# Six preparation tasks and two gate rows moved from the end of the input projection into attention steps 6 to 25

## The chip, the cores and the metric

The kernel runs on one core of one Trainium2 chip. The metric is the device time of one execution in microseconds (us). The core's engines are named as in the profile: PE (TensorE, matrix products; PEld its weight loads), DVE (VectorE), ACT (ScalarE), POOL (GpSimd) and SP (SyncE, which here only issues DMAs). Each engine works through its own queue in order. ACT issues DMAs as well, out of the same queue as its arithmetic.

## The reference

One step of a one-layer encoder over 1024 prompt frames and 32 sample frames, 1056 rows in all, in fp32, with a width of 1024:

```python
h = rmsnorm(x, g_mix)
q, k, v, cb, cc, cx, ga, gc = split(h @ w_in)        # 3 x 512, 3 x 512, 2 x 1024 columns
y_attn = stick_breaking(q, k, v) @ w_attn_out         # 8 heads x 64, strictly causal
y_conv = (cb * causal_conv(cc * cx)) @ w_conv_out
merged = sigmoid(ga) * y_attn + sigmoid(gc) * y_conv
x = x + merged @ w_o
x = x + square(relu(rmsnorm(x, g_ffn) @ w_up)) @ w_down
x = x + sigmoid(rmsnorm(x, g_ple) @ w_ple_gate) * (p @ w_ple)
y = rmsnorm(x, g_final)
# stick_breaking: A[t,s] = beta[t,s] * prod over s<j<t of (1 - beta[t,j]), beta = sigmoid(q k / 8)
```

The outputs are `y` and the new keys, values and convolution rows. The sample frames attend to 256 cached frames as well.

## The kernel before

Activations lie with features on the 128 partitions and the 1056 rows in the free dimension. A product in fp32 precision is made of three faster ones: each operand is split into a high part (a cast on ACT to `fp32r`) and a low part (the rest, a subtraction on DVE), and high x high, high x low and low x high are summed in PSUM. The larger products are cut into 2 x 2 blocks and done with seven block products in place of eight (`seven`).

The stages follow one another: input projection (column sets `SETS`, 0 to 17), attention, the two branches with their gates, output projection, MLP up and down, and the last gated addition. PE has work in nearly all of it. The order on ACT, PE, DVE and POOL is that of the program text (`manual_schedule(engines=MM)`); DMAs issued on SP are placed by the framework.

**The input projection.** `run(seven(...))` makes one set of two 128-column blocks; at each of its `yield`s every generator in the list `side` is advanced by one piece. `after(n, g)` lets n turns go by first. The last set, 17, is gate rows 6 and 7; `last_m` keeps its two tiles unscaled. A short piece of other PE work (`START`) and the rest of `side` follow, and then the attention.

**The six tasks.** `ahead_gate(n)` (n = 4, 5) loads raw gate row n from `gd`, lets four more turns go by, multiplies it by the row norm `rs` (`scaled`, DVE, 128x1056), takes the sigmoid on ACT, and stores it to `gs_` with a DMA that ACT issues. `ahead_attn(n)` (n = 4 to 7) loads weight row n of `w_attn_out` (256 KB), splits it some turns later (ACT cast and DVE subtraction, 128x512), and two turns after that stores both halves to `aod` (512 KB, issued by ACT). The branches read `gs_` and `aod` after the attention.

**The attention.** The prompt is done in 64 steps: 4 pairs of heads x 2 heads x 8 blocks of 128 queries. Step n with block i = n mod 8 has 128(i+1) keys. The loop `for n in range(LAST + 3)` runs a pipeline over three steps, in the order `ORDER = "LSAFBFG"`:

- L: DVE scan along the keys of step n-1 (`weigh`, `remains`), and leftovers of `pending`
- S: `scores(n)`: PE products into the PSUM tile `z`, which has one buffer; sigmoid on ACT from `z` to `r` (L865); POOL sets the masked corner of `r`
- A and B: `flip(n-2)`: PE transposes of `r`, high part by ACT (L918), low part by DVE (L919), into tiles `at`
- F: other PE work (gate rows 0 to 3, embedding, convolution branch), cut into pieces; `shares()` allots it to the steps beforehand
- G, in odd blocks: `gather(n-3)`, PE products of weights and values into `av`

At the top of an even step SP gets the loads of the queries for step n+4 (`queries`, three DMAs), and at i = 2 the keys and values of the next head (`keys_values`). Steps 1 to 14 carry the sample frames' attention too (`sample_loads`, `samples`).

In the kernel before, the two kept rows of `last_m` are scaled at the top of steps 3 and 4, and pass the sigmoid and are stored at the top of steps 5 and 6.

Most large tiles, operands, gate rows, `at`, keys and values, the tiles of the six tasks and the kept rows, share one pool, `bpool`, with `NBUF = 34` buffers of 128 x 1056 fp32.

Of the kernel before, what the change touches and what calls it, by code (L numbers as in the profile page):

```python
# [11 lines left out]
AF = mybir.ActivationFunctionType  # L12
# [32 lines left out]
ORDER = "LSAFBFG"  # L45
START = 2.5
SQ_AT = 96
AHEAD = 6
MM = {mybir.EngineType.Activation, mybir.EngineType.PE, mybir.EngineType.DVE, mybir.EngineType.Pool}


# [1 line left out]
def tile_step(  # L53
# [8 lines left out]
    nc = tc.nc  # L62
# [7 lines left out]
    def blk(name, dt=F32, shape=None):  # L70
        return bpool.tile(shape or [P, T], dt, tag="B", name=name)
# [13 lines left out]
    for m_, a_, b_ in ((keep, 1.0, 0.0), (drop, 0.0, 1.0)):  # L85
        nc.gpsimd.memset(m_, a_)
        for p_ in range(4):
            r_ = m_[32 * p_ : 32 * p_ + 32, :]
            nc.gpsimd.affine_select(
                r_, r_, pattern=[[-1, DEC]], compare_op=ALU.is_gt, fill=b_, base=0, channel_multiplier=1  # L90
# [51 lines left out]
    raws, ws, side = {}, {}, []  # L142
# [174 lines left out]
    def after(n, *gens):  # L317
        for _ in range(n):
            yield
        for g in gens:  # L320
            yield from g

    def call(f, *a):
        f(*a)
        yield

    def run(body):

        for _ in body:
            for g in list(side):  # L330
                if next(g, g) is g:
                    side.remove(g)
# [4 lines left out]
    SETS = [("g", 12), ("g", 4)] + [(nm, 0) for nm in ("cc", "cx", "cb", "q", "k", "v")] + [("g", 8)]  # L337
# [115 lines left out]
    def stats_x():  # L453

        nc.vector.memset(ssq, 1.0)
        for i in range(9):
            n = P if i < 8 else DEC
            r = rows[i % 3][:n, :]
            nc.scalar.activation(r, r, AF.Square, accum_out=ssq[:n, i : i + 1])
            if i < 6:  # L460
                load_rows(i + 3)
            for _ in range(3 if i in (2, 5) else 1):
                yield
        nc.scalar.activation(rst, ssq, AF.Sqrt, bias=eps_t, scale=1.0 / D)
        nc.vector.reciprocal(rst, rst)
        for _ in range(3):
            yield
        for q0 in (0, 3, 6):
            spread(rst, rs, q0)


    gd = dpool.tile([16, P, T], F32, name="gd")
# [53 lines left out]
    def scaled(m, by=None):  # L526
        if by is None:
            dve(m, m, rs, op=ALU.mult)
        else:
            nc.vector.scalar_tensor_tensor(m, m, by, rs, op0=ALU.mult, op1=ALU.mult)  # L530
# [97 lines left out]
    def ahead_attn(n):  # L628
        t = blk(f"ao{n}", F32R, [P, 2, 4, P])
        raw = t[:, 1].bitcast(F32)  # L630
        nc.sync.dma_start(raw, w_attn_out[n])
        for _ in range(5):
            yield
        nc.scalar.copy(t[:, 0], raw)
        dve(t[:, 1], raw, t[:, 0].bitcast(F32), op=sub)
        yield
        yield
        nc.scalar.dma_start(aod[n], t.bitcast(F32).rearrange("p e k n -> p e (k n)"))
        yield

    def ahead_gate(n):
        m = blk(f"ga{n}")
        nc.sync.dma_start(m, gd[n])
        for _ in range(5):
            yield
        scaled(m)
        yield
        nc.scalar.activation(m, m, AF.Sigmoid)
        nc.scalar.dma_start(gs_[n - 4], m)
        yield  # L650
# [55 lines left out]
    def second_parts(a):  # L706

        r = blk(f"xb{a}", F32, [P, 2, TH])
        for i in range(2):
            nc.sync.dma_start(r[:, i, :], xf[4 * a + 2 * i][:, TH:])  # L710
        for _ in range(4):
            yield
        for i in range(2):
            j = 2 * a + i
            d, g = operand("B12", j), gmix[:, 2 * j : 2 * j + 1]
            nc.scalar.activation(d[:, 0, :], r[:, i, :], AF.Copy, scale=g)
            mix(d[:, 1, :], r[:, i, :], g, d[:, 0, :].bitcast(F32), sub)
            yield
# [125 lines left out]
    def queries(p, j, c):  # L844
        q = live["q", p, j, c] = apool.tile([P, 2, 256], F32R, tag="Q", name=f"q{p}{j}{c}", bufs=3)
        src = qd[p, 64 * j : 64 * j + 64, :, c * 256 : (c + 1) * 256]
        nc.sync.dma_start(q[0:64, :, :].bitcast(F32), src)
        nc.sync.dma_start(q[64:128, 0, :].bitcast(F32), src[:, 1, :])
        nc.sync.dma_start(q[64:128, 1, :].bitcast(F32), src[:, 0, :])
# [36 lines left out]
    def weigh(p, j, i):  # L886
        remains(*live[p, j, i])
# [337 lines left out]
    with tc.manual_schedule(engines=MM):  # L1225
        nc.scalar.preload_act_table_set("sqrt_and_others")
        run(first_gates())
        for s_ in range(2, len(SETS)):
            nm, n = SETS[s_]
            if s_ == 2:  # L1230
                side.append(after(1, stats_x()))
            elif s_ == 4:
                nc.scalar.preload_act_table_set("sigmoid_and_others")
            elif s_ == len(SETS) - 1:
                side.extend(after(AHEAD + i // 2, ahead_gate(n)) for i, n in enumerate((4, 5)))
                side.extend(after(AHEAD + 1 + i // 2, ahead_attn(n)) for i, n in enumerate(range(4, 8)))
            if s_ + 1 < len(SETS):
                side.append(prepare(f"i{s_ + 1}", AT_IN))
            else:
                side.extend([after(4, second_parts(0)), after(6, second_parts(1)), after(4, call(hooks_to, -20)), after(10, call(hooks_to, 0))])  # L1240
            if s_ + 2 < len(SETS):
                side.append(after(5, call(fetch_in, s_ + 2)))
            m = blk(f"m1_i{s_}"), blk(f"m2_i{s_}")
            run(seven(f"i{s_}", *m, copy_of))
            if s_ + 1 < len(SETS):
                follow(nm, n, m, 6 * (s_ == 2))
            else:
                last_m = n, m
        keys_values(0, 0)
        pools[:] = [gps]  # L1250
        run(ahead(START))
        while side:
            run(range(1))
# [99 lines left out]
    with tc.manual_schedule(engines=MM):  # L1353
        queries(0, 0, 0)
        queries(0, 0, 1)
        for n in range(LAST + 3):
            done_f, parts = 0, None
            if n in (3, 4):
                scaled(last_m[1][n - 3])
            elif n in (5, 6):  # L1360
                m = last_m[1][n - 5]
                nc.scalar.activation(m, m, AF.Sigmoid)
                nc.scalar.dma_start(gd[last_m[0] + n - 5], m)
            if n == 1:
                sample_loads()
            elif n == 3:
                sample_keys()
            if n < LAST:
                i = steps[n][2]
                if i % 2 == 0 and n + 4 < LAST:  # L1370
                    p_, j_, i_ = steps[n + 4]
                    queries(p_, j_, i_ // 2)
                if i == 2 and n + 8 < LAST:
                    keys_values(*steps[n + 8][:2])
            for op in ORDER:
                if op == "S" and n < LAST:
                    scores(*steps[n])
                    if n == LAST - 1:
                        zf = zps.tile([P, 2, 512], F32, tag="z", name="zf")
                        spare_ps.extend(zf[:, h, :] for h in range(2))  # L1380
                elif op == "L":
                    if 1 <= n <= LAST:
                        weigh(*steps[n - 1])
                    for f in pending + split_low:
                        f()
                    pending.clear()
                    split_low.clear()
                elif op == "F" and n < LAST + 2:
                    done_f += 1
                    fill(share[n] + (share[n + 1] - share[n]) * done_f / nf)  # L1390
                    if done_f == 1 and n in SAMPLE_AT:
                        next(sample, None)
                elif op == "G" and n >= 3 and steps[n - 3][2] % 2 == 1:
                    p, j, i_ = steps[n - 3]
                    gather(p, j, i_ // 2)
                elif op in "AB" and 2 <= n <= LAST + 1:
                    if op == "A":
                        parts = flip(*steps[n - 2])
                    next(parts, None)
            for p, c in splits.get(n, ()):  # L1400
                split_high(p, c)
            branches_ahead(n)
            if n == LAST + 1:
                fill(2 * total)
                hooks_to(len(plan))
                split_high(3, slice(0, 768))
        for f in pending + split_low:
            f()
        split_high(3, slice(768, T))
        split_low.pop()()  # L1410
# [997 lines left out]
```

## Time and profile before

| | us |
|---|---|
| median of 3 runs | 1540.46 |
| lowest, highest | 1539.76, 1541.39 |
| profiled execution, its own time | 1543.13 |
| span of the profiled execution | 1541.4 |

| stretch of the profiled execution | from, to (us) |
|---|---|
| issue of the loads of the six tasks (SP) | 384.6 to 390.3 |
| their arithmetic (DVE, ACT) | 396.3 to 403.8 |
| first and last scores on PE | 403.0, about 605 |
| scores of step 8 | 434.6 |

The span runs from the first instruction's start to the last one's end. Rows of a timeline are: start, duration, engine, line, operation, output tile <- inputs, shape; a bracket gives the time for which the engine stood idle before it and what ended that. "DMA" in a row of stretches is the busy share of the 16 DMA engines.

### The profile page before, as it was taken

What the parts mean: (1) busy time and instruction counts of PE and PEld (TensorE: products, weight loads), DVE (VectorE), ACT (ScalarE), POOL (GpSimd) and SP (SyncE); (2) the same over time, 40 slices, a digit from 0 to 9 for tenths busy, and PEclk for the clock granted to TensorE, in tenths of its full rate; (3) what the DMA queues carried; (4) which work ended last, traced back from release to release, by engine and by line L of the source; (5) the groups of instructions that cost most, each with busy time, mean ns of one, the idle gap of its engine ahead of it and who ended that gap; (6) DMA issues with size and microseconds to landing.
All of it is one profiled execution on the core that took longest, in us unless ns stands there. A gap on an engine that the chain in (4) does not pass through costs nothing.

```text
span 1541.4 us, 29904 instructions
## 1 busy us (share of the span) xinstructions
PE 1511.6 (98%) x11888; PEld 1498.2 (97%) x11888; DVE 1131.5 (73%) x1597; ACT 763.0 (50%) x1415; POOL 280.9 (18%) x318
## 2 busy tenths in 40 slices
PE   8999999999899999999999999999999999999997
PEld 8999999999789999999999999999999999999997
DVE  7568666657578988799876677675576986799756
ACT  6544444434456666333375556645543334434654
POOL 2123322231012212000002113222020220000253
PEclk9999999999999999999999999999999999999999
DMA  6513445413946752446755455544886897673443
GB/s 223 202 51 114 190 153 193 166 45 132 311 133 191 253 164 92 168 162 224 267 182 173 159 171 209 193 154 154 300 282 200 277 332 240 205 274 121 140 127 118
DMA packets 121036, 286.83 MB, mean 186 GB/s; under 512 B 13856, under 2 KB 34592, under 8 KB 120896
## 3 DMA queue, kind: packets, MB, share of 16 engines
q1 hardware_dynamic: 119456, 280.34, 54.3%
q10 hardware_dynamic: 1440, 4.58, 0.7%
q8 instruction: 93, 1.52, 0.4%
q14 instruction: 47, 0.39, 0.1%
HBM read 200.98 MB, written 83.89 MB: 185 GB/s over the span
## 4 chain that ended last, share of the span: by engine, by line
PE 59%; DVE 2%; ACT 1%; issue 1%; DMA 0%; SPq 0%; DVEq 0%; ACTq 0%
PE ps_dn L1993 7%; PE ps_dn L1991 7%; PE ps_dn L1992 7%; PE ps_woA L1709 4%; PE ps_A11u L244 2%; PE ps_A11u L242 2%; PE ps_A11u L243 2%; PE ps_pg L120 2%; PE ps_pg L121 2%; PE ps_pg L122 2%; PE ps_S1u L243 2%; PE ps_S1u L244 2%; PE ps_S1u L242 2%; PE ps_woS L1709 2%; PE ps_oa L120 1%; PE ps_oa L122 1%
## 5 line engine op out<-in xcount | busy, mean ns | idle before, releaser
L1993 PE MATMUL ps_dn<-fh,wlo_dn 128*128 128x264 f32 x896 | 255.4, 285 | 0.0
L1992 PE MATMUL ps_dn<-fl,whi_dn 128*128 128x264 f32 x896 | 254.9, 284 | 0.0
L1991 PE MATMUL ps_dn<-fh,whi_dn 128*128 128x264 f32 x896 | 254.8, 284 | 0.0
L1991 PEld LDWEIGHTS ps_dn<-fh,whi_dn 128*128 128x128 f32 x896 | 168.9, 188 | 0.0
L1993 PEld LDWEIGHTS ps_dn<-fh,wlo_dn 128*128 128x128 f32 x896 | 168.8, 188 | 0.0
L1992 PEld LDWEIGHTS ps_dn<-fl,whi_dn 128*128 128x128 f32 x896 | 168.6, 188 | 0.0
L209 POOL TENSOR_TENSOR s_u<-raw_u,raw_u 128x512 f32<-128x512 f32 x22 | 32.1, 1461 | 359.6 <-DVE slS_u L170 284.6
L879 DVE TENSOR_TENSOR_SCAN r<-r 128x128 f32<-128x128 f32 (+3 forms) x64 | 86.5, 1351 | 2.8 <-POOL r L872 2.8
L209 POOL TENSOR_TENSOR s_i<-raw_i,raw_i 128x512 f32<-128x512 f32 x32 | 44.2, 1380 | 239.4 <-DVE slS_i L170 210.3
L1878 ACT CAST whi_dn<-raw_dn 128x1024 fp32r<-128x1024 f32 x40 | 42.0, 1051 | 84.9 <-PE ps_dn L1992 80.9
L1884 DVE TENSOR_TENSOR wlo_dn<-raw_dn,whi_dn 128x1024 fp32r<-128x1024 f32 x40 | 60.9, 1523 | 29.0 <-ACT whi_dn L1878 28.9
L919 DVE TENSOR_TENSOR at<-pa,at 128x512 fp32r<-128x512 f32 (+2 forms) x96 | 52.0, 550 | 31.5 <-ACT at L918 26.9
L242 PE MATMUL ps_A11i<-T,shS_i 128*128 128x264 f32 x256 | 73.1, 286 | 0.0
L244 PE MATMUL ps_A11i<-T,slS_i 128*128 128x264 f32 x256 | 73.0, 285 | 0.0
L243 PE MATMUL ps_A11i<-T,shS_i 128*128 128x264 f32 x256 | 72.8, 284 | 0.0
L170 DVE TENSOR_TENSOR slS_i<-s_i,shS_i 128x512 fp32r<-128x512 f32 x48 | 34.8, 731 | 50.0 <-ACT shS_i L168 49.9
L1904 DVE TENSOR_TENSOR fl<-mr,fh 128x1056 fp32r<-128x1056 f32 x56 | 69.9, 1247 | 0.0
L1753 ACT ACTIVATE m<-m 128x528 f32<-128x528 f32 (+1 forms) x52 | 31.8, 611 | 74.6 <-DVE m L289 30.4
L872 POOL TENSOR_SCALAR_AFFINE_SELECT r<-r 128x128 f32<-128x128 f32 x64 | 30.4, 475 | 201.6 <-ACT r L865 191.4
L2075 POOL TENSOR_TENSOR xx<-xx,pgs 128x384 f32<-128x384 f32 (+1 forms) x23 | 24.2, 1056 | 216.5 <-DVE pgs L2074 209.9
L170 DVE TENSOR_TENSOR slS_u<-s_u,shS_u 128x512 fp32r<-128x512 f32 x48 | 34.3, 715 | 39.8 <-ACT shS_u L168 39.8
L1899 ACT CAST fh<-mr 128x1056 fp32r<-128x1056 f32 x56 | 60.1, 1073 | 0.3 <-DMA mr<-mdB 0.3
(568 smaller groups left out, 5699.0 us busy)
## 6 DMA issues: line engine op xcount, KB each, us to landing
raw_dn<-in_w_down_dram SPq DMA_DIRECT2D x56, 512.0 KB, 4.7
raw_i<-in_w_in_dram SPq DMA_DIRECT2D x36, 512.0 KB, 4.5
mr<-mdT SPq DMA_DIRECT2D x32, 528.0 KB, 5.5
raw_u<-in_w_up_dram SPq DMA_DIRECT2D x32, 512.0 KB, 3.7
mr<-mdB SPq DMA_DIRECT2D x24, 528.0 KB, 6.0
mdB<-m SPq DMA_DIRECT2D x44, 264.0 KB, 2.7
raw_pg<-in_w_ple_gate_dram SPq DMA_DIRECT2D x17, 512.0 KB, 3.6
mdT<-ta SPq DMA_DIRECT2D x32, 264.0 KB, 2.1
```

Source lines behind the costliest of these rows:

```text
L170: dve(l, src, h.bitcast(F32), op=sub)
L209: f()
L242: nc.tensor.matmul(p_, wh[:, k, :], o[:, 0, c], start=new and n == 0, stop=False, **on)
L243: nc.tensor.matmul(p_, wh[:, k, :], o[:, 1, c], start=False, stop=False, **on)
L244: nc.tensor.matmul(p_, wl[:, k, :], o[:, 0, c], start=False, stop=z, **on)
L879: nc.vector.tensor_tensor_scan(rev, rev, rev, 1.0, ALU.mult, ALU.bypass)
L1709: nc.tensor.matmul(on, w[:, i, :], o, start=new and i == n == 0, stop=i == 3 and n == 2, skip_group_check=True,)
L1884: dve(lo, raw, hi.bitcast(F32), op=sub)
L1904: dve(l, mraw.pop(v), opd[v].bitcast(F32), op=sub)
L1991: nc.tensor.matmul(ps, hi[:, j, :], oh, start=j == 0, stop=False)
L1992: nc.tensor.matmul(ps, hi[:, j, :], ol, start=False, stop=False)
L1993: nc.tensor.matmul(ps, lo[:, j, :], oh, start=False, stop=j == NP_ - 1)
```

## The change

The six tasks leave the list `side` of the last projection set and are begun inside the attention loop: each is advanced by one piece at the top of every step from the one that `LINES` gives. A gate row that is begun at step n is loaded at n, scaled at n+5, and passes the sigmoid and is stored at n+6; a weight row is loaded at n, split at n+5 and stored at n+7. The two kept rows are scaled at steps 12 and 20 (`KEEP_AT`), and pass the sigmoid and are stored two steps later. The arithmetic and the bytes moved stay the same.

```diff
-AHEAD = 6
+LINES = {6: ("g", 4), 8: ("a", 4), 10: ("a", 5), 14: ("g", 5), 16: ("a", 6), 18: ("a", 7)}
+KEEP_AT = (12, 20)
...
-            elif s_ == len(SETS) - 1:
-                side.extend(after(AHEAD + i // 2, ahead_gate(n)) for i, n in enumerate((4, 5)))
-                side.extend(after(AHEAD + 1 + i // 2, ahead_attn(n)) for i, n in enumerate(range(4, 8)))
...
+        lines = []
         for n in range(LAST + 3):
             done_f, parts = 0, None
-            if n in (3, 4):
-                scaled(last_m[1][n - 3])
-            elif n in (5, 6):
-                m = last_m[1][n - 5]
-                nc.scalar.activation(m, m, AF.Sigmoid)
-                nc.scalar.dma_start(gd[last_m[0] + n - 5], m)
+            if n in LINES:
+                k_, r_ = LINES[n]
+                lines.append((ahead_gate if k_ == "g" else ahead_attn)(r_))
+            for g in lines:
+                next(g, None)
+            for i_, at_ in enumerate(KEEP_AT):
+                m = last_m[1][i_]
+                if n == at_:
+                    scaled(m)
+                elif n == at_ + 2:
+                    nc.scalar.activation(m, m, AF.Sigmoid)
+                    nc.scalar.dma_start(gd[last_m[0] + i_], m)
```

## The prediction

> **What bounds the kernel now.** I read the page first, then the rows of TensorE (PE) in order of time, then what else is in that stretch.
>
> ```profile
> span 1541.4 us, 29904 instructions
> PE 1511.6 (98%) x11888; PEld 1498.2 (97%) x11888; DVE 1131.5 (73%) x1597; ACT 763.0 (50%) x1415; POOL 280.9 (18%) x318
> ```
>
> PE is busy in 98% of the span, so the kernel runs at the pace of PE's queue, and time is to be won only where PE stands still or is clocked down. From the timeline of PE between 388 and 445 us, these are the only rows that report an idle time (in brackets: us idle, and who ended it); the fourth line of the fence after it is the longest wait of PE from 430 to 620 us, the rest of the attention.
>
> ```profile
> 395.72 0.39 PE L729 MATMUL ps_g<-B,whi_g 128*128 128x264 f32 x1 [1.23 <-ACT m_i L721]
> 403.04 0.30 PE L861 MATMUL z<-ks,q 128*128 128x128 f32 x1 [1.07 <-ACT ao L634]
> 410.12 0.58 PE L861 MATMUL z<-ks,q 128*128 128x256 f32 x1 [4.35 <-ACT r L865]
> 426.25 0.74 PE L861 MATMUL z<-ks,q 128*128 128x448 f32 x1 [2.66 <-ACT r L865]
> ...
> PE av L936 <- DVE at L919: 1.2, 2, 0.6
> ```
>
> Four stops of 1.23 + 1.07 + 4.35 + 2.66 = 9.31 us lie together around the start of the attention; behind them nothing waits longer than 0.6 us at a time. The rows of 4 us stretches (busy us and instructions of PE, PEld, DVE, ACT, POOL; granted clock; DMA share; GB/s) show a second loss there.
>
> ```profile
> 392.00:396.00 4.00, 2.77 (x23) 2.56 (x21) 1.97 (x3) 2.57 (x4) 0.00 (x0) 1.00 1.09 326
> 404.00:408.00 4.00, 1.77 (x15) 1.56 (x13) 0.71 (x1) 1.32 (x2) 0.00 (x0) 1.00 0.82 296
> 408.00:412.00 4.00, 1.88 (x8) 1.88 (x9) 1.20 (x3) 0.66 (x2) 0.58 (x2) 0.61 0.84 281
> 412.00:416.00 4.00, 4.00 (x19) 3.85 (x18) 1.51 (x3) 1.49 (x7) 0.58 (x3) 0.54 1.05 400
> 424.00:428.00 4.00, 1.75 (x5) 1.48 (x6) 1.30 (x2) 2.27 (x3) 0.29 (x1) 0.74 0.91 310
> 428.00:432.00 4.00, 4.00 (x27) 3.78 (x26) 3.21 (x4) 2.37 (x6) 0.58 (x3) 0.83 0.53 196
> ```
>
> After the 4.35 us stop the granted clock is 0.61 and 0.54, after the 2.66 us stop 0.74 and 0.83, and 1.00 in between. If the reduced clock is one half, the four rows hold 8 x (0.39 + 0.46 + 0.26 + 0.17) = 10.24 us of it. PE was still standing in some of that: it begins about 408.9 (0.39 x 8 = 3.1 us before 412) and 425.9 (2.1 before 428), and PE starts at 410.12 and 426.25, so 8.6 us of work ran at half speed and lost 4.3 us. The place costs 9.31 + 4.3 = 13.6 us.
>
> Why PE stops is in ACT's rows of the same stretch. ACTq are DMAs that ACT issues; they stand in ACT's queue in order.
>
> ```profile
> 393.10 0.74 ACT L716 ACTIVATE B<-xb,vecT 128x528 fp32r<-128x528 f32 x1 [7.67 <-PE ps_A11i L244]
> ...
> 403.21 2.96 ACTq L638 DMA_DIRECT2D aod<-ao  x2
> 406.21 1.04 ACT L111 CAST whi_g<-raw_g 128x1024 fp32r<-128x1024 f32 x1 [2.93 <-DMA aod<-ao]
> ...
> 407.38 2.37 ACTq L638 DMA_DIRECT2D aod<-ao  x2
> 409.79 0.28 ACT L865 ACTIVATE r<-z 128x128 f32<-128x128 f32 x1 [2.26 <-DMA aod<-ao]
> ...
> 421.29 1.08 ACT L1362 ACTIVATE m_i<-m_i 128x1056 f32<-128x1056 f32 x1
> 424.96 0.33 ACTq L1363 DMA_DIRECT2D gd<-m_i  x1
> 425.39 0.81 ACT L865 ACTIVATE r<-z 128x768 f32<-128x768 f32 x1 [3.01 <-DMA q<-qd]
> ```
>
> A store issue takes 0.33 us (424.96). The two pairs of weight stores took 2.96 and 2.37: in each the second stood until an earlier DMA had landed. The kept gate row's store was ready at 422.4 and went out at 424.96, after a q load had landed. Behind these stands the sigmoid of the scores (L865), and `z` has one buffer, so the next scores wait for that sigmoid: the 4.35 and the 2.66 us stops. ACT's DMAs wait that long because the DMA engines are full. From the DMA view of 380 to 430 us (count, KB each, median us to landing), and as the last line the same q loads in 435 to 490 us:
>
> ```profile
> DMA packets 7054, 14.82 MB, mean 296 GB/s; under 512 B 803, under 2 KB 3867, under 8 KB 7050
> ...
> aod<-ao ACTq DMA_DIRECT2D x4, 512.0 KB, 5.5
> ga<-gd SPq DMA_DIRECT2D x2, 528.0 KB, 6.8
> gs__158<-ga ACTq DMA_DIRECT2D x2, 528.0 KB, 5.8
> gd<-m_i ACTq DMA_DIRECT2D x2, 528.0 KB, 5.0
> ao<-in_w_attn_out_dram SPq DMA_DIRECT2D x4, 256.0 KB, 7.5
> q<-qd SPq DMA_DIRECT2D x12, 64.0 KB, 5.1
> xb<-in_xf_dram SPq DMA_DIRECT2D x2, 264.0 KB, 6.8
> ...
> q<-qd SPq DMA_DIRECT2D x16, 64.0 KB, 2.6
> ```
>
> The first five of these groups are the moved work: 4 x 512 + 2 x 528 + 2 x 528 + 2 x 528 + 4 x 256 = 6240 KB, about 6.3 of the 14.82 MB. With them the q loads take 5.1 us to land; later, without, 2.6.
>
> **The change part by part. Taken out of the end of the input projection:** two gate rows (load, scale, sigmoid, store) and four weight rows (load, high part, low part, store).
>
> ```profile
> L528 DVE TENSOR_TENSOR ga<-ga,rs x2: 1249/1250/1250, 396.3 to 397.4; 128x1056 f32<-128x1056 f32 x2
> L648 ACT ACTIVATE ga<-ga x2: 1087/1088/1089, 397.6 to 399.1; 128x1056 f32<-128x1056 f32 x2
> L634 ACT CAST ao<-ao x4: 615/617/621, 400.5 to 402.4; 128x512 fp32r<-128x512 f32 x4
> L635 DVE TENSOR_TENSOR ao<-ao x4: 684/688/693, 401.2 to 403.1; 128x512 fp32r<-128x512 f32 x4
> L528 DVE TENSOR_TENSOR m_i<-m_i,rs x2: 1248/1248/1249, 415.1 to 417.5; 128x1056 f32<-128x1056 f32 x2
> ```
>
> Their DVE time there (2 x 1.25 + 4 x 0.69 = 5.3 us) and ACT time (2 x 1.09 + 4 x 0.62 = 4.7) are beside PE work and not themselves the loss; the stores and the 6.3 MB are. What goes, stop by stop. The 4.35 us stop: no store is left ahead of the first sigmoid, and ACT's other work there (a cast of 1.04 and two copies) is ready before it; gone, and its half clock with it. The 2.66 us stop: the kept row's store moves from step 5 to 14; gone with its half clock. The 1.07 us stop is put down to an `ao` cast that the scores don't need, so it is the landing of the first q and ks loads; those were issued behind the moved loads and land sooner; I take all. The 1.23 us stop hangs on ACT's L716, which starts at 393.10 on the `xb` load (PE had long been done); that load stands on SP behind the two gate loads and took 6.8 us; at 5 or less PE no longer sees it. Sum: 9.31 + 4.3 = 13.6 us less, the most that I can see. If only the two long stops go, 7.0 + 4.3 = 11.3.
>
> **What may be late next at the start.** With ACT free, the first steps go at PE's pace, so the loads for steps 4 to 6 (q, the sample's cache tiles, ks and vv of the next head) are needed 8 to 13 us sooner, over DMA engines that still have 14.82 - 6.3 = 8.5 MB in that stretch. At 296 GB/s this is 29 us of transfers in some 40: no longer full, but it comes in bursts. Bounds: 0, if landing falls to 2.6 us; one more stop like the one at 426.25 with its half clock (0.5 x 3.05 = 1.5), 4.2, if landing stays at 5.1. I take 1.5, nearer the quiet row, since 42% of the bytes go.
>
> [...]
>
> **Put into the attention.** Each task yields five times after its load, so gate rows are scaled at steps 11 and 19, weight rows split at 13, 15, 21 and 23, kept rows scaled at 12 and 20; the eight stores go out at 12, 14, 15, 17, 20, 22, 23 and 25. Step 8 of the old run is here, and then stretches by steps (8 to 10, 11 to 15, 16 to 18, 19 to 23):
>
> ```profile
> 434.99 0.28 ACT L865 ACTIVATE r<-z 128x128 f32<-128x128 f32 x1 [0.32 <-PE z L862]
> ...
> 434.60:444.90 10.30, 9.65 (x80) 9.13 (x79) 10.23 (x20) 4.69 (x13) 2.11 (x8) 1.00 0.44 136
> 444.90:463.10 18.20, 18.20 (x164) 17.30 (x163) 11.70 (x15) 10.43 (x23) 2.19 (x10) 1.00 0.27 85
> 463.10:471.90 8.80, 8.80 (x76) 8.77 (x76) 8.41 (x12) 4.62 (x13) 1.71 (x7) 1.00 0.59 168
> 471.90:485.60 13.70, 13.70 (x106) 13.20 (x106) 10.80 (x15) 8.44 (x17) 2.04 (x9) 1.00 0.57 184
> ```
>
> DVE, by group of steps: 1.25 + 1.25 + 0.69 + 0.69 = 3.9 us more in steps 11 to 15, where 18.2 - 11.7 = 6.5 are free: nothing. The same 3.9 in steps 19 to 23, where 2.9 are free: short by 1.0. Bounds 0 to 1.0; I take 0.5, as DVE may run behind PE by part of a step. No heavy piece falls on the full steps 8 to 10 and 16 to 18. ACT gains 2.2 + 1.2 + 1.1 us a group over 7.8 and 5.3 free: nothing by sum.
>
> Queues: ACT issues eight stores (0.33 each) ahead of a step's flips and sigmoid. Each may again wait for an earlier DMA, with L865 behind it and then PE; the DMA share of these steps is 0.27 to 0.59 and the landing 2.6 us, and a step gives ACT about 2 us before PE asks for its sigmoid. SP issues six loads more ahead of a step's q loads, which are four steps early. `bpool` has 34 buffers: counting live tiles at step 8 (rs, 16 operand tiles, 3 of keys and values, 3 of the sample, a gate row in the making, oT, 2 + 4 at tiles) I get 31 now; with two kept rows, `ga` and `ao` 35, so one `at` tile or load waits there until the step's gather. Bounds of stores and buffers together: 0, and 4.2 us (a stop like that of 426.25). I take 1.0, near the lower end, by the DMA share.
>
> **Sum:** -13.6 + 1.5 + 0.5 + 1.0 = -10.6 us. The profiled execution took 1543.13 us with a span of 1541.4, 2.7 over the median of 1540.46; I take the difference off the median: 1529.9.
>
> **Rivals.** (A) The start stays short of loads: two of the steps 1 to 6 stop as at 426.25, 2 x 4.2 us, in place of the 1.5. For it: 8.5 MB remain, and q and cache loads are in small pieces (3867 of 7054 packets under 2 KB). Against: landing halves where the DMA is not full. Time: -13.6 + 8.4 + 0.5 = -4.7, 1535.8. (B) The work comes back in the attention: DVE's 1.0 short, and two or three stops by buffers and stores, 10 to 13 us in all: 1538 to 1541, within 0.2%. For it: steps 8 to 10 have DVE at 10.23 of 10.3, and 35 buffers are wanted. Against: no DVE piece falls there. (C) Slower, by the stores alone: an ACT store waits for a load that SP, itself held by a full pool, has not yet issued, and ACT stands for the landing. At 4.2 us a store, it eats the gain from the fourth of eight on; with five, -13.6 + 21 = +7.4, 1547.9. For it: this is what happened at 424.96. Against: it takes a full DMA, which these steps have not.
>
> **How the numbers follow.** My forecast 0.68, A 0.16, B 0.09, C 0.07. The predicted time is the forecast's. Its own range is 1526.9 (all 13.6, nothing new) to 1533.5; to hold 8 in 10 the range takes in A and reaches 1537.4, where B begins, and a little under the ceiling, 1526. About 0.2% (3.1 us) is what can be told from no change: faster than 1537.4 has the forecast and A, 0.84; within it B, 0.09; slower C, 0.07.
>
> **What would show it.** Right: no idle over 1 us on PE between 390 and 430 us, the granted clock 1.00 through the first eight steps, step 8 starting some 11 to 13 us sooner than 434.6, q loads there landing in about 3 us, PE's pace from steps 8 to 25 as before within 2 us, and behind the attention the same lengths. Wrong: a clock under 1 near the first steps (A), idle on PE before `z` or `av` in steps 8 to 25 (B), ACT waiting behind its stores there (C).

## The result, and the profile after

| | before | changed |
|---|---|---|
| median | 1540.93 us (4 runs) | 1529.52 us (4 runs) |
| lowest, highest | 1539.76, 1543.95 | 1529.03, 1529.73 |
| span of the profiled execution | 1541.4 | 1527.8 |

The ratio is 0.9923 with a 95% interval of 0.9905 to 0.994: 12 us less, between 9 and 15. The forecast was 1529.9. The two profiled spans differ by 13.6 us, more than the medians do, because the kernel before varies: its 29 runs beside the first experiments lie between 1539.79 and 1545.83 us, and its profiled execution, at 1543.13, is one of the longer ones. The changed kernel's four runs lie within 0.7 us. One execution each of two experiments (e4, e6) and of the changed kernel run again (e11) took 3811.99, 2981.3 and 2090.83 us; these three stand in no ratio below.

The page's first lines, and all waits of PE between 395 and 490 us (most line numbers are 1 to 5 higher than before, those of the sample's products 2 lower):

```profile
span 1527.8 us, 29906 instructions
PE 1507.0 (99%) x11888; PEld 1494.6 (98%) x11888; DVE 1131.3 (74%) x1597; ACT 763.5 (50%) x1415; POOL 285.1 (19%) x318
...
PE pa L916 <- DVE r L880: 0.8, 1, 0.8
PE av L937 <- DVE at L920: 0.7, 1, 0.7
```

The four stops of 1.23, 1.07, 4.35 and 2.66 us are gone; what is left is a wait of 0.8 us at step 17, which is new, and 0.7 us at step 10, which was there before. The rows of 4 us stretches at the old place:

```profile
392.00:396.00 4.00, 4.00 (x35) 4.00 (x34) 1.28 (x3) 0.76 (x2) 0.00 (x0) 1.00 0.14 49
...
404.00:408.00 4.00, 4.00 (x32) 3.83 (x31) 2.61 (x5) 2.40 (x10) 0.88 (x4) 1.00 0.98 247
408.00:412.00 4.00, 4.00 (x43) 3.36 (x42) 2.96 (x4) 3.31 (x9) 0.59 (x3) 1.00 0.99 273
412.00:416.00 4.00, 4.00 (x33) 3.89 (x33) 2.76 (x3) 2.57 (x6) 0.88 (x4) 1.00 1.01 334
```

PE is busy in all of each, at a granted clock of 1.00. The DMA share is still about 1 between 404 and 416 us. What changed is how much stands ahead of the loads that PE needs, as the DMA view of 380 to 430 us shows (it now reaches step 10, with about 1 MB of the moved loads in it):

```profile
DMA packets 6269, 10.42 MB, mean 208 GB/s; under 512 B 752, under 2 KB 4336, under 8 KB 6263
...
q<-qd SPq DMA_DIRECT2D x16, 64.0 KB, 3.1
...
xb<-in_xf_dram SPq DMA_DIRECT2D x2, 264.0 KB, 4.7
...
kk<-in_ckT_dram SPq DMA_DIRECT2D x4, 128.0 KB, 3.6
```

The q loads land in 3.1 us (5.1 before), `xb` in 4.7 (6.8). Step 8 starts at 420.0 in place of 434.6, 14.6 us sooner, where 11 to 13 were forecast. Then by the stretches of the prediction (steps 8 to 10, 11 to 15, 16 to 18, 19 to 23):

```profile
420.00:430.30 10.30, 9.64 (x80) 9.17 (x79) 10.23 (x20) 4.68 (x13) 2.19 (x8) 1.00 0.61 194
430.30:448.40 18.10, 18.10 (x163) 17.20 (x162) 13.68 (x16) 13.37 (x26) 4.94 (x10) 1.00 0.77 242
448.40:458.20 9.80, 9.01 (x76) 8.77 (x75) 9.67 (x15) 4.80 (x13) 1.72 (x8) 1.00 0.67 201
458.20:472.00 13.80, 13.80 (x107) 13.28 (x106) 12.94 (x16) 11.51 (x21) 5.57 (x9) 1.00 0.94 284
```

Their lengths were 10.3, 18.2, 8.8 and 13.7 us. Only the third grew, by 1.0, and all of that is step 17. From there to the end the two executions run in step: -14.6 + 1.0 = -13.6 us, the difference of the spans.

### The profile page after: what moved, and what is told of

It is laid out like the page before. It is cut to its first block, busy times and chain, and to the rows that moved or that the text cites. A ratio compares the mean times of both kernels' runs of the same rounds, so it can differ in the third digit from the quotient of the medians.

```text
span 1527.8 us, 29906 instructions
## 1 busy us (share of the span) xinstructions
PE 1507.0 (99%) x11888; PEld 1494.6 (98%) x11888; DVE 1131.3 (74%) x1597; ACT 763.5 (50%) x1415; POOL 285.1 (19%) x318
## 4 chain that ended last, share of the span: by engine, by line
PE 59%; DVE 2%; ACT 1%; issue 1%; DMA 0%; SPq 0%; DVEq 0%; ACTq 0%
PE ps_dn L1998 7%; PE ps_dn L1996 7%; PE ps_dn L1997 7%; PE ps_woA L1714 4%; PE ps_A11u L243 2%; PE ps_A11u L245 2%; PE ps_A11u L244 2%; PE ps_pg L121 2%; PE ps_pg L122 2%; PE ps_pg L123 2%; PE ps_S1u L243 2%; PE ps_S1u L244 2%; PE ps_S1u L245 2%; PE ps_woS L1714 2%; PE ps_oa L123 1%; PE ps_oa L121 1%
## 5 line engine op out<-in xcount | busy, mean ns | idle before, releaser
L873 POOL TENSOR_SCALAR_AFFINE_SELECT r<-r 128x128 f32<-128x128 f32 x64 | 35.1, 549 | 180.2 <-ACT r L866 173.7
L920 DVE TENSOR_TENSOR at<-pa,at 128x512 fp32r<-128x512 f32 (+2 forms) x96 | 51.7, 549 | 18.4 <-ACT at L919 13.6
```

## The experiments

Two theories could explain the gain, and the prediction used both together. **Q**: the stores that ACT issues stand in ACT's queue ahead of the scores' sigmoid. **D**: 6.3 MB in a full stretch make the loads that PE needs late, whoever issues them. All ratios are to the kernel before on the same chip, in five rounds.

### Each half of the change alone

The kept gate rows alone (`e1_kept_only`) and the six tasks alone (`e2_tasks_only`):

```diff
 # e1, in the kernel before; the six tasks stay in side
-            if n in (3, 4): ...
-            elif n in (5, 6): ...
+            for i_, at_ in enumerate((12, 20)): ...
 # e2, in the changed kernel
-            for i_, at_ in enumerate(KEEP_AT): ...
+            if n in (3, 4): ...
+            elif n in (5, 6): ...
```

> The kernel before with only the two kept gate rows moved (scaled at steps 12 and 20, stored at 14 and 22); the six tasks stay at the end of the input projection. Theory Q (ACT's queue stands behind the stores that it issues): the stop at step 5 goes with its half clock, 2.66 + 1.5 = 4.2 us less than before, the stops ahead of step 2 stay. Theory D (6.3 MB too many in the DMA engines make the loads late, whoever issues the stores): 5.2 of the 6.3 MB are still there, so the place of the stop is taken by a late load, 0 to 1.5 us less than before.

> The changed kernel with the two kept gate rows back at steps 3 to 6; the six tasks stay in the attention. Theory Q: a store in ACT's queue ahead of the scores' sigmoid costs there what it cost, so 4.2 us are missing from the gain of the changed kernel: about 9 us less than before. Theory D: with 5.2 MB gone the load that the store waits for has landed already, the store goes out in 0.33 us and the whole gain is there: within 1 us of the changed kernel, 11 to 13 us less than before.

Measured: e1 1540.57 us, ratio 0.9986 (0.9977 to 0.9995); e2 1531.15 us, ratio 0.9926 (0.9914 to 0.9938). The six tasks carry the gain; the kept rows alone bring 2.2 us (0.8 to 3.5), and on top of the tasks at most 1 to 2: the changed kernel did not run on this chip, and its ratio elsewhere, 0.9923, can't be told from 0.9926. In e2 the kept rows' stores are where they were, at steps 5 and 6. The first three rows are ACT's in e2, the last is PE's in e1:

```profile
411.08 1.09 ACT L1366 ACTIVATE m_i<-m_i 128x1056 f32<-128x1056 f32 x1
412.19 0.35 ACTq L1367 DMA_DIRECT2D gd<-m_i  x1
412.65 0.81 ACT L866 ACTIVATE r<-z 128x768 f32<-128x768 f32 x1 [0.48 <-ACT m_i L1366]
...
425.16 0.44 PE L861 MATMUL z<-ks,q 128*128 128x448 f32 x1 [1.01 <-DMA q<-qd]
```

Before, this store stood 2.6 us behind its sigmoid; here it goes out at once, from the same place in the queue, as D says. In e1, with the six tasks' bytes still there, the 2.66 us stop is gone, as Q says, and a stop of 1.01 us for a late q load has come in its place, as D says; the first long stop took 6.56 us in that execution. The 2.2 us of e1 lie between the two forecasts. So that stop needed both: a store ahead of the sigmoid, and the traffic that holds the store up.

### The same bytes, issued by SP

```diff
-        nc.scalar.dma_start(aod[n], ...)          # likewise gs_ and the kept rows
+        nc.sync.dma_start(aod[n], ...)
```

> The kernel before with all eight stores (four of aod, two of gs_, two of the kept rows) issued by SP instead of ACT; nothing else moves, the same bytes go at the same place. Theory Q: ACT is free, the two long stops and the half clock go, the 1.23 and 1.07 us stops stay: 11.3 us less than before. Theory D: the DMA engines are as full as before and SP now stands behind the stores with its q loads: at most 4 us less than before, and PE waits for q or ks loads in steps 0 to 6.

Measured: 1539.68 us, ratio 0.9984 (0.9976 to 0.9993), 2.5 us of the 11.3 that Q gives. The first row is from PE's timeline, the second from the waits of SP's queue between 384 and 440 us:

```profile
409.96 0.45 PE L861 MATMUL z<-ks,q 128*128 128x128 f32 x1 [5.45 <-DMA q<-qd]
...
SPq L649 <- ACT ga L648: 4.9, 1, 4.9
```

ACT is free and a stop is there again, now ahead of the very first scores: SP waits 4.9 us for the `ga` sigmoid that its store needs, with q loads behind it. The first of these goes out at 404.70 us, in the kernel before at 396.43. So it is not enough to take the stores out of ACT's queue. This does not show D: the q loads issued here up to 412 us land in 2.8 us (4.8 before), so they are late because they are issued late. The stand has only moved to SP.

### Bytes without the queue, and the queue without the bytes

```diff
 # e6, in the changed kernel: ten stores of 528 KB to spare_rows, which nobody reads
+                side.extend(after(6 + i // 2, call(lambda i=i: nc.sync.dma_start(spare_rows[i], done_m[i % 2]))) for i in range(4))
...
+            if n < 2:
+                for i_ in range(3):
+                    nc.sync.dma_start(spare_rows[4 + 3 * n + i_], last_m[1][1])
 # e7, in the changed kernel: six stores of 16 KB to spare_cols, which nobody reads
+                for i, at_ in enumerate((13, 13, 15, 15, 16, 16)):
+                    side.append(after(at_, call(nc.scalar.dma_start, spare_cols[i], keep)))
```

> The changed kernel with bytes put back at the old place and nothing else: SP stores ten more rows of 528 KB that nobody reads, four (2.1 MB) during the last projection set and six (3.2 MB) in steps 0 and 1, behind the first two q loads. ACT issues no store before step 12. Theory D (bytes in the DMA engines): the q, ks and cache loads land in 5 us or more as before, PE stops in steps 0 to 6, and 5 us or more of the 12 us gain are lost. Theory Q (ACT's queue behind its stores): ACT has none there, the gain stays within 2 us.

> The changed kernel with six stores of 16 KB that nobody reads, issued by ACT at the old places of the six tasks' stores (two behind the last projection copy, four ahead of the first scores' sigmoid): the place in ACT's queue without the bytes. Theory Q: each pair waits for earlier DMAs as before, PE stops ahead of the scores of step 1, 4 us or more are lost. Theory D: earlier DMAs have landed already, each goes out in 0.33 us, and the time is that of the changed kernel within 1 us.

Measured: e6 1537.13 us, ratio 0.9966 (0.9954 to 0.9978), so 7 to 8 us of the gain are lost; e7 1529.12 us, ratio 0.9915 (0.99 to 0.993), nothing lost. In e6 the one stop of PE in the start, and the cache loads in the DMA view of 380 to 430 us:

```profile
413.89 2.27 PE L1275 MATMUL zs<-kk,qs 64*32 64x288 f32 x16 [5.71 <-DMA kk<-in_ckT_dram]
...
cv<-in_cache_v_dram SPq DMA_DIRECT2D x1, 512.0 KB, 7.3
kk<-in_ckT_dram SPq DMA_DIRECT2D x4, 128.0 KB, 5.9
```

The sample's products of step 4 wait 5.71 us for `kk`, which stands behind the extra stores; it is not one of the four old stops, and the q loads, forecast at 5 us or more, land in 4.2. The granted clock falls to one half there for 3.4 us (its mean over the execution is 0.997, in the changed kernel 0.998). In e7 ACT's queue, with the stores at their old places:

```profile
393.74 0.82 ACTq L325 DMA_DIRECT2D spare_cols<-keep  x2
...
399.60 1.79 ACTq L325 DMA_DIRECT2D spare_cols<-keep  x4
401.52 0.28 ACT L867 ACTIVATE r<-z 128x128 f32<-128x128 f32 x1 [1.54 <-DMA spare_cols<-keep]
```

Four stores go out in 1.79 us, where four took 2.96 + 2.37 us around a cast before, and the sigmoid behind them is on time. The place in ACT's queue without the bytes costs nothing; the bytes without that place cost most of the gain. But e6 puts its bytes into SP's queue ahead of the cache loads, and by an estimate its loss is mostly that: the first `kk` load is issued at 406.91 us, in the changed kernel at 401.11, and lands 6.9 us after its issue, in the changed kernel 3.6. With the slower landing alone it would have come at 408.05, and PE stops at 408.18. So e6 shows what these stores cost at that place, not what a slower transfer alone costs.

The traces hold what ties the two theories together. Each DMA names the semaphore (a counter) that its landing raises. In the kernel before all 794 DMAs, those of SP and ACT together, take eight semaphores in turn, and none goes out before the earlier one with its semaphore has landed, so at most eight are in flight; it is the same in the changed kernel. The q load that shares a semaphore with the kept row's store landed at 424.88 us, and the store goes out at 424.96; each of the four weight stores goes out 0.08 us after such a landing too. Of the DMAs issued between 384 and 430 us, 19 go out within 0.1 us of such a landing in the kernel before, 14 of SP and 5 of ACT, and none in the changed kernel. So bytes that land late hold up whichever queue issues next: ACT with its sigmoid behind the store, or SP with its loads. The 16 KB stores of e7 land in 1.5 to 3.8 us, and the places come free in time.

### The half clock alone

In the kernel before, products of constants fill the 4.35 us stop and keep PE busy; 27 of them in e4, 13 in e8:

```diff
             if n == 1:
+                pd = tps.tile([P, 512], F32, tag="tp", name="ps_dummy")
+                for _ in range(27):                # 13 in e8
+                    nc.tensor.matmul(pd[:, :P], ones, ones, start=True, stop=True)
                 sample_loads()
```

> The kernel before with 27 products of 128 x 128 constants, about 0.11 us each and 3.0 us together, put on PE ahead of the scores of step 1, where it stands 4.35 us; their result is not used. If the half clock after that stop costs time by itself, the granted clock stays at 1.00 there and 2.8 us go (5.6 us of work from 410.1 to 415.7 at half speed). Rival: the work of steps 1 to 3 waits for ACT and the loads whatever the clock: no change, within 0.5 us.

> The kernel before with 13 products of constants ahead of the scores of step 1 instead of 27. With 27, the profile shows two passes of 0.115 us each for every product, 6.2 us together, so that PE came to the scores of step 1 later than before; 13 take 3.0 us and fit into the stop. If the half clock costs by itself: clock 1.00 through steps 1 to 4, step 8 some 2.5 us sooner than before and the same in the time. If what comes next (sample loads at step 4, the store at step 5) takes it back: step 5 starts sooner, step 8 and the time do not change by more than 1 us.

Measured: e4 1544.0 us, ratio 1.0014 (1.0005 to 1.0023); e8 1543.18 us, ratio 1.0006 (0.9997 to 1.0015). In e4 the products took 6.2 us, twice what I had counted, and reached past the stop. In e8 they fit. Stretches of steps 1 to 3, 4 and 5, first in the kernel before, then in e8:

```profile
410.10:417.00 6.90, 6.88 (x33) 6.66 (x34) 3.20 (x5) 2.61 (x10) 1.23 (x6) 0.60 1.05 384
417.00:420.80 3.80, 3.80 (x41) 3.19 (x40) 3.80 (x6) 2.75 (x8) 0.94 (x4) 1.00 0.98 229
420.80:426.20 5.40, 2.78 (x22) 2.54 (x20) 1.39 (x2) 2.31 (x5) 0.00 (x0) 0.97 1.01 292
...
411.30:415.70 4.40, 4.40 (x34) 4.23 (x35) 2.52 (x5) 2.65 (x10) 1.26 (x6) 1.00 1.00 385
415.70:421.10 5.40, 5.08 (x41) 3.40 (x40) 5.40 (x7) 2.83 (x8) 1.59 (x4) 1.00 1.05 259
421.10:426.40 5.30, 2.82 (x23) 2.58 (x21) 0.65 (x2) 2.38 (x5) 0.00 (x0) 1.00 1.02 260
```

At the full clock steps 1 to 3 take 4.4 us in place of 6.9: the 2.5 us of half-clock loss are real (in rows of 1 us the granted clock of the kernel before is 0.50 from 409 to 415 us). But step 1 began 1.2 us later in this execution, step 4 takes 5.4 in place of 3.8, step 5 is as long as before with the kept row's store in it, and step 6 starts at 426.4 against 426.2. In step 4 the sample's products wait for `kk` loads and end at 419.9 us, against 419.6 before: what comes next is bound by its loads, whatever the clock did. The mean granted clock of the profiled execution is 0.995 in the kernel before, 0.997 in e8, and 0.998 in e4 and in the changed kernel. By an estimate from these four, e8 keeps the half clock of the stop ahead of step 6, and only the first of the two stretches at half clock was taken away.

### The rest of step 17 and step 10

```diff
 # e5: weight row 5 begun at step 20 in place of 10
-LINES = {..., 10: ("a", 5), ..., 18: ("a", 7)}
+LINES = {..., 18: ("a", 7), 20: ("a", 5)}
 # e9: the sample's parts earlier; e10: e9 with weight row 5 begun at step 23
-    SAMPLE_AT = {4: 1, 8: 1, 9: 1, 10: 1, 11: 1, 12: 1, 14: 1}
+    SAMPLE_AT = {4: 1, 5: 1, 8: 1, 9: 1, 11: 1, 12: 1, 14: 1}
```

> The changed kernel with one of the six tasks, weight row 5, begun at step 20 instead of 10, so that it is split at step 25 instead of 15. In the changed kernel PE waits 0.79 us for a scan at step 17 and that step takes 3.58 us against 2.58 before. If DVE carries a backlog of the tasks out of steps 11 to 15, the 0.69 us less there shortens step 17 by most of that 1.0 us: 0.7 to 1.0 us less than the changed kernel, 12.5 less than before. If the wait comes from something else at step 17, the time is that of the changed kernel within 0.3 us.

> The changed kernel with the sample attention's parts called at steps 4, 5, 8, 9, 11, 12, 14 instead of 4, 8, 9, 10, 11, 12, 14: its first scan and product on DVE (1.6 us) leave step 8 for step 5, where the changed kernel's DVE has 1.6 us free, and the second pair leaves step 9 for 8. PE's only stop of steps 8 to 10 (0.66 us in the changed kernel and the kernel before, ahead of the gather of step 10) hangs on DVE's at. If DVE's backlog makes it, step 10 gets 0.7 to 1.0 us shorter, and the time is 0.5 to 1.0 us under the changed kernel. If the DVE work is only moved into a step as full, the stop moves with it and the time is the same within 0.3 us.

> The same with weight row 5 begun at step 23 (split at 28, stored at 30): not at 20, where its load stood between two ACT stores and the second then waited 1.75 us for the first to land. Step 17 takes 2.58 us again, no ACT store waits, and steps 20 to 30 keep the changed kernel's lengths: 0.7 to 1.0 us under the run without it, 1.5 to 2.0 under the changed kernel. Rival: as with the row begun at 20, what step 17 gives comes back at another step: the time of the run without it within 0.3 us.

> The changed kernel once more, as the measure for the two runs beside it on the same chip: 11 to 12 us less than before.

Measured: e5 1529.03 us, ratio 0.9914 (0.99 to 0.9927); e9 1530.01, 0.9918; e10 1529.26, 0.9916; the changed kernel beside them 1529.58, 0.9916 (0.9901 to 0.9932). None beats it by what can be told.

In e5 step 17 takes 2.58 us again, so the backlog on DVE that this row left was its cause. But the first row here (PE) is a stop that was not there, and the others (ACT) say why:

```profile
467.79 0.50 PE L862 MATMUL z<-ks,q 128*128 128x512 f32 x1 [0.72 <-ACT r L866]
...
463.54 1.10 ACT L1367 ACTIVATE m_i<-m_i 128x1056 f32<-128x1056 f32 x1
466.39 0.33 ACTq L1368 DMA_DIRECT2D gd<-m_i  x1
466.82 0.92 ACT L866 ACTIVATE r<-z 128x896 f32<-128x896 f32 x1 [2.18 <-DMA gs__158<-ga]
```

A store ready at 464.64 goes out at 466.39, when the gate row's store with the same semaphore has landed (466.32), and the sigmoid and the next scores wait behind it: rival C of the prediction, at 0.7 us of PE. Step 26, behind the split at step 25, is 0.9 us longer as well. In e9 step 10 is 1.0 us shorter and step 9 0.6 longer. In e10 steps 17 to 28 give the 1.0 us, and the stretch of steps 29 to 32 takes it back (first the changed kernel, then e10):

```profile
485.30:499.70 14.40, 14.24 (x113) 13.74 (x112) 14.27 (x17) 10.73 (x22) 3.31 (x9) 1.00 1.01 312
...
483.20:498.60 15.40, 14.57 (x112) 13.59 (x112) 15.27 (x18) 11.07 (x22) 5.50 (x11) 1.00 1.03 334
```

DVE is busy in 14.27 of 14.4 and in 15.27 of 15.4 us: it has no room, and the stretch grows by as much as step 17 had given.

## Why the prediction was right, and where not

**The place and the size.** The 13.6 us ceiling (9.31 of stops and 4.3 of half clock) was read from one stretch, and that stretch gave 14.6 us. All four stops went, the clock stayed at 1.00. The 1.0 us more lies ahead of step 1, whose scores begin at 410.12 and 402.51 us, 7.6 apart, with 6.65 us of reported stops. A stop cost more than its reported idle time: ahead of the 1.23 us stop the same products of PE lie 0.1 us apart in the two executions, the fourth product behind it 1.7 (396.31 and 394.61).

**New costs, 3.0 in the sum, 1.0 measured.** Late loads at the start, taken as 1.5: none; PE has no stop between 395 and 425 us. With them rival A, two more stops, fell. Stores and buffers, taken as 1.0: none; no ACT store made PE wait, though at step 8 I had counted 35 tiles for 34 buffers. Steps 8 to 10 are as long as before. DVE, taken as 0.5 at steps 19 to 23: 1.0, and elsewhere. I let steps 11 to 15 off because DVE had 6.5 us free there; but free time spread over a group was not time in which a step's pieces were ready, and a backlog reached step 17. The scan that began 1.3 us into step 16 before begins 2.7 us into it now (451.14 against a start at 448.4).

**Two causes in one step.** "No store is left ahead of the first sigmoid" and "the kept row's store moves from step 5 to 14" were given as what removes the long stops. The place in the queue alone was not it: small stores at that place cost nothing (e7), the kept row's store left at its place doesn't stop PE once the six tasks are gone (e2). It was a part of it, since with the tasks in place the 2.66 us stop went with that store (e1). The sentence that carries the gain was the one after: ACT's DMAs wait that long because the DMA engines are full (a DMA share of 0.82 to 1.05 in its rows of 404 to 416 and 424 to 428 us). What it lacked is that SP's loads wait in the same way, for one of eight DMAs in flight to land, as 14 of them did between 384 and 430 us. Freeing ACT's queue alone was worth 2.5 us and not 11.3 (e3), as SP then stood in its place.

**The half clock as a term of its own.** I added 4.3 us to 9.31 as if either could go alone. Taking 2.5 us of it away alone gained nothing (e8); in the changed kernel steps 1 to 3 take 4.3 us, and step 4, with its loads there, stays at 3.8. Nor is the half clock a fixed part of such a stop, as the 4.2 us for one in the prediction has it. A stop of 2.84 us at the same place in e4 left the clock at 1.00 (a row of PE, and the stretch behind it):

```profile
426.44 0.48 PE L861 MATMUL z<-ks,q 128*128 128x448 f32 x1 [2.84 <-ACT r L865]
...
426.40:430.00 3.60, 3.56 (x25) 3.40 (x26) 2.62 (x3) 3.14 (x6) 0.88 (x4) 1.00 0.94 352
```

The length of a stop alone does not tell whether the clock falls: in e6 a stop of 5.71 us has 3.4 us of half clock with it, in the kernel before one of 2.66 us has 3.4 us, and the longer one of 2.84 us in e4 has none. What decides it, these runs do not show.

**The range.** Forecast and measurement differ by 0.4 us because errors cancel, which is luck. Between the two profiled executions the gain was 13.6 us and the sum 10.6: 2.0 too much for new costs, 1.0 too little for the start. (Rival A's sum leaves out the 1.0 for stores and buffers; with it A would be 1536.8.) But the profiled execution of before, which the sum describes, is 2.2 us longer than its kernel's median, and the changed one is not.

## What to carry to other kernels

Where an engine stands behind a DMA that it issues, ask first what that DMA waits for: with transfers in flight far beyond what the next steps need, moving the work and its bytes out of that stretch gained 12 us, while moving the stores to another queue gained 2.5. Look up how many DMAs the program lets be in flight (here eight). Try the suspected wait and the suspected load each alone, as e7 does; together they look like one cause. A run that puts the load back must not put it ahead of the loads that it is to slow, as e6 did. In a stretch where two engines are nearly full, a piece that is moved takes its cost along: three tries to move pieces of 0.7 to 1.6 us, against waits of 0.8 and 0.7 us, gained nothing.

## What the runs showed that I had not expected

A DMA share near 1 was not in itself a loss: the changed kernel has 0.98 to 1.01 from 404 to 416 us, and PE does not stop. The moved work raises the share of steps 11 to 15 from 0.27 to 0.77 and of steps 19 to 23 from 0.57 to 0.94; the first group is 0.1 us shorter than before, the second 0.1 longer.

The changed kernel is also steadier: its eight runs that stand in the ratios, in two rounds, lie within 0.7 us, against 6 us over 29 runs before. The stops of the old start differed from one profiled execution to the next: 4.35 us ahead of step 1 in the first, 6.56 in e1, whose program differs only from step 3 on.
